# A hybrid attention block: hand order in the Fourier-projection stage, contiguous query columns for the maxima, block ends ahead on VectorE

## The chip, the cores and the metric

The kernel runs on one core of one Trainium2 chip. The metric is the device time of one execution in microseconds (us): the median of three runs before the change is 3602.55 us (3600.46 to 3602.69). The engines are called PE (TensorE; PEld is its weight loading), DVE (VectorE), ACT (ScalarE), POOL (GpSimd) and SP (SyncE, which issues nearly all DMAs).

## The reference

Two layers act on 2048 latent tokens and 256 context tokens of width 1024, in float32. Cut to what matters here:

```python
def layer(x, ctx, c, c_ctx, p, row, col, update_ctx):
    hx = rmsnorm(x, p["norm_g"]) * (1.0 + sc[:, None, :]) + sh[:, None, :]
    px = jnp.split(hx @ p["w_in"], SPLIT_IDX, axis=-1)      # ctx likewise: pc
    qa_x, ka_x, va_x, qb_x, kb_x, vb_x = attn_features(px, p, row, col)
    att_a = attend(qa_x, concat([ka_x, ka_c]), concat([va_x, va_c]))   # MLA, 4 heads
    att_b = attend(qb_x, concat([kb_x, kb_c]), concat([vb_x, vb_c]))   # GQA, 4 heads
    x_new = x + gt[:, None, :] * merge(px, att_a, att_b, p)

def attend(q, k, v):
    s = einsum("bqkgd,blkd->bkgql", q, k) * dk ** -0.5
    return einsum("bkgql,blkd->bqkgd", softmax(s), v)

def merge(parts, att_a, att_b, p):
    ya = att_a * silu(ga); yb = att_b * silu(gb)
    yc = chunk_mlp(u, vc, p) * silu(gc)
    yd = fourier(f, p["fnet_w"]) * silu(gd)          # 2-D FFT, then a matrix
    return concat([ya, yb, yc, yd]) @ p["w_out"]
```

The context tokens are updated in the first layer only, and read only context.

## The kernel before

**Projections.** A layer first runs the normed input through its projections, in two halves of the tokens (`HALVES`; the last one has token blocks 2 and 3, of 512 tokens). Matmuls are split in a high and a low part, three for each product (lines 364 to 366 and 714 to 716). The last stage of a half is `stage_f`: for each token block it multiplies two weight tiles (`load_coltile`, line 343: DMA of two pieces each on SP, cast on DVE, low part on POOL) with the input, 24 matmuls a tile, and then four times 6 matmuls by the Fourier matrix of the columns, whose results go to DRAM (`Z`).

**Attention** has 16 blocks a layer: four pairs of heads (0, 1 MLA; 2, 3 GQA) by four blocks of 512 queries. A block takes 18 steps over 128 keys. A step is 10 score matmuls (GQA 8; line 1140), exponentials on ACT (line 1148) and sums of `p` on POOL (line 1159, with the steps of the set `dve` on DVE); every third step 12 matmuls of `p` with the values (line 1126). The scores' last pair of matmuls has 33 rows: the 33rd carries the query's maximum, so that the exponential needs none. These maxima are found ahead: during block n the 18 *max units* of block n+1 run (`max_units`, line 963; `fill`). Sixteen are chunks, with 4 matmuls (GQA 2) of 128 queries by 512 keys into two PSUM banks "m" (line 976), which DVE reduces (line 988); two are tails over the 256 context keys, after which `mt` is complete for half the queries (lines 995, 1000). `row()` (line 1016) then writes `mt` as a row into the query tile `qt` by DMAs on SP.

**Order.** In attention the order on PE, DVE, POOL and ACT is that in which the code is written (`tc.manual_schedule`); elsewhere a scheduler sets it, and it sets SP's everywhere. PE, DVE, POOL, ACT and SP each run their instructions in order. The max units of a layer's first block are given to the second `stage_f` (`fill`), under the scheduler's order. Block 0's units end with the stage; block 3's units (for block 4) need the keys of pair 1, loaded by SP at that time (lines 953 to 957).

**The end of a block.** `join` adds DVE's sum to POOL's (line 1179), `fin` makes the denominators (line 1196) and sends them through DRAM, `recip` (line 1209) and `fin2` (line 1216) run on DVE steps later. In blocks 0 to 2 DVE also does the Fourier branch (`fu`, with 32 matmuls at line 854 each time). After the last block the output projection begins, whose weights and inputs share stage buffers with POOL's and DVE's work (lines 1321, 1322, 1338 to 1340).

Of the kernel before, what the change touches and what calls it, by code (L numbers as in the profile page):

```python
# [15 lines left out]
P = 128  # L16
# [20 lines left out]
def kernel(  # L37
# [49 lines left out]
    def f32(ap):  # L87
        return ap.bitcast(F32)
# [270 lines left out]
            nc.tensor.matmul(pt[:, :n], hx(0, k)[:, js], lo(k), start=False, stop=False)  # L359
            nc.tensor.matmul(pt[:, :n], hx(1, k)[:, js], hi(k), start=False, stop=(k == KD - 1))  # L360

    def feat_major(pt, hx, wt, n):
        for k in range(KD):
            nc.tensor.matmul(pt[:, :n], wt[:, 0, k, :], hx(0, k), start=(k == 0), stop=False)  # L364
            nc.tensor.matmul(pt[:, :n], wt[:, 0, k, :], hx(1, k), start=False, stop=False)  # L365
            nc.tensor.matmul(pt[:, :n], wt[:, 1, k, :], hx(0, k), start=False, stop=(k == KD - 1))  # L366
# [17 lines left out]
    def layer(l, xin, shs, hxs, xss, c):  # L384
# [300 lines left out]
                sg = silu2(pg, n, hx_p.tile([P, 512], F32, tag="t", name="sg"))  # L685
                load(G[gi][:, t0:t0 + n], sg[:, :n])

        def stage_f(hxs, blks, fill):
            left = [4 * len(blks)]

            def drain():
                k = -(-len(fill) // left[0])
                left[0] -= 1
                for u in fill[:k]:
                    u()
                del fill[:k]
            wts = [load_coltile(l, 2144 + P * i) for i in range(2)]
            for b in blks:
                t0, n = blk_tokens(b)
                fT = []  # L700
                for i in range(2):
                    pf = bank("s", [P, 512])
                    feat_major(pf, hxs[b], wts[i], n)
                    f = wk("f", [P, 2, 512], F32R, bufs=3)
                    nc.scalar.copy(f[:, 0, :n], pf[:, :n])
                    nc.vector.tensor_tensor(f[:, 1, :n], pf[:, :n], f32(f[:, 0, :n]), op=ALU.subtract)
                    fT.append(f)
                    drain()
                for j in range(n // P):
                    pz = bank("o", [P, 512])  # L710
                    js = slice(j * P, (j + 1) * P)
                    for i in range(2):
                        f, w = fT[i], c.aw
                        nc.tensor.matmul(pz, f[:, 0, js], w[:, 0, i, :], start=(i == 0), stop=False)
                        nc.tensor.matmul(pz, f[:, 0, js], w[:, 1, i, :], start=False, stop=False)
                        nc.tensor.matmul(pz, f[:, 1, js], w[:, 0, i, :], start=False, stop=(i == 1))
                    zt = wk("zt", [P, 512], bufs=3)
                    nc.scalar.copy(zt, pz)
                    load(Z[:, t0 // P + j, :], zt)
                    if j % 2 == 1 and b < 4:  # L720
                        drain()

        def fnet_load():
            zt = []
# [240 lines left out]
        def max_units(blk, qt):  # L965
# [6 lines left out]
            def mm(pm, c0, qi, s0, n):  # L972
                seq = (0, 2) if pair < 2 else (0,)
                for sel in seq:
                    for e in range(2):
                        nc.tensor.matmul(  # L976
                            pm[e][:, c0:c0 + n], qt[64 * e:64 * e + 64, sel, qi:nq:nqt],
                            kp.kk(e, sel, 64, s0, n), start=(sel == 0), stop=(sel == seq[-1]),
                        )

# [32 lines left out]
            def row():  # L1013
                for e in range(2):
                    r = 64 * e + 32
                    load(
                        f32(qt)[r:r + 1, 3 if pair < 2 else 2, :nq].rearrange("r (p x) -> r p x", x=nqt),
                        f32(mt)[:, 4 * e:4 * e + nqt],
                    )
            return units, row  # L1020

        blocks = [(pair, qb) for pair in range(4) for qb in range(4)]
# [12 lines left out]
        def merge(x, y):  # L1035
# [6 lines left out]
                i = j  # L1042
            return r + x[i:]

        for hi_, half in enumerate(HALVES):
            full = [b for b in half if not (last and b == 4)]
            wc = load_c((nc.scalar.copy, nc.vector))
            if c is None:
                c = consts(l)
            for b in half:  # L1050
                if b not in hxs:
                    hxs[b] = make_hx(b, shs, xin, xss.get(b))
            with scope(f"c{l}{hi_}"):
                stage_c(hxs, full, wc)
                if hi_ == 0:
                    make_up(l, c)
                wm = load_group(l, (0, 352), 2)
            with scope(f"m{l}{hi_}"):
                wg, pre = group_units(l, (608, 1120), 2)
                stage_mla(hxs, half, wm, pre)  # L1060
            with scope(f"g{l}{hi_}"):
                wg0 = load_coltile(l, GC[0])
                stage_gqa(hxs, half, wg)
            with scope(f"t{l}{hi_}"):
                mods, shs_next = [], None
                if hi_ == 1:
                    gt, mods = mods_b(l, 1 if last else 2)
                    if not last:
                        shs_next, more = mods_a(l + 1)
                        mods += more  # L1070
                for gi in range(6):
                    ws = mods[gi][0]() if gi < len(mods) else None
                    stage_gate(hxs, full, gi, wg0 if gi == 0 else None)
                    if ws:
                        mods[gi][1](ws)
                    if gi == 0 and hi_ == 0:
                        make_aw(l, c)
                if hi_ == 1:
                    load_kc()
                    first_max = prep_block(0)  # L1080
                    fill = first_max[2][0] + [first_max[2][1]]
                else:
                    hxs[2] = make_hx(2, shs, xin)
                    fill = []
                stage_f(hxs, full, fill)
        c.pool.__exit__(None, None, None)

        def attention():
# [148 lines left out]
            for n, (pair, qb) in enumerate(blocks):  # L1237
# [9 lines left out]
                if n >= 3:  # L1247
                    dve = {(i, 1) for i in range(0, 15, 3)}
                    if pair >= 2:
                        dve |= {(i, 1) for i in range(1, 16, 3)}  # L1250
                if n == 5:
                    load_v2()
                own, zc = [], None
                if not last and qb == 3:
                    own, zc = ctx_units(pair)
                z = main_units(blk, qt, dve)
                done = 0
                for i in range(18):
                    z.scores(i)
                    want = min(len(fill), -(-len(fill) * (i + 1) // 16))  # L1260
                    while done < want:
                        fill[done]()
                        done += 1
# [4 lines left out]
                        own.pop(0)()  # L1268
                    if i % BATCH == BATCH - 1:
                        z.sums(i)  # L1270
                        j = n * 6 + i // 3
                        mults = [m() for m in fmm]
                        fmm = []
# [6 lines left out]
                        if mults and not fu and not fmm:  # L1280
                            ffin()
                        z.sums2()
                        if i == 2 and prev:
                            prev.join()
                        if tail:
                            tail.pop(0)()
                        if i == 5 and prev:
                            prev.fin()
                            tail += prev.tail
# [9 lines left out]
            for f in prev.tail:  # L1299
                f()  # L1300

        ordered = {
            mybir.EngineType.PE, mybir.EngineType.DVE, mybir.EngineType.Pool, mybir.EngineType.Activation
        }
        banks_close()
        banks_open(f"pa{l}", s=4, m=3, o=1)
        with scope(f"a{l}"), tc.manual_schedule(engines=ordered):
# [209 lines left out]
```

## Time and profile before

| | |
|---|---|
| median of 3 runs | 3602.55 us |
| the profiled execution | 3604.51 us, its span 3602.7 us |
| PE busy | 3344.2 us (93%), PEld 2415.1 us (67%) |
| DVE, POOL, ACT busy | 1981.9 us (55%), 1862.5 us (52%), 1246.8 us (35%) |
| the chain that ended last, by engine | PE 29%, DVE 6%, DMA 2%, issue 2%, POOL 1%, ACT 1% |
| mean granted clock of PE | 0.963 |

The span is what the hardware profiler saw of one execution. Busy shares are averages over stages: PE is near full in the steady part of attention and in the projections, and leaves gaps at the seams between stages and blocks. The granted clock is 1.0 at 2.4 GHz and 0.5 at 1.2 GHz.

### The profile page before, as it was taken

What the parts mean: (1) busy time and instruction counts of PE and PEld (TensorE: products, weight loads), DVE (VectorE), ACT (ScalarE), POOL (GpSimd) and SP (SyncE); (2) the same over time, 40 slices, a digit from 0 to 9 for tenths busy, and PEclk for the clock granted to TensorE, in tenths of its full rate; (3) what the DMA queues carried; (4) which work ended last, traced back from release to release, by engine and by line L of the source; (5) the groups of instructions that cost most, each with busy time, mean ns of one, the idle gap of its engine ahead of it and who ended that gap; (6) DMA issues with size and microseconds to landing.
All of it is one profiled execution on the core that took longest, in us unless ns stands there. A gap on an engine that the chain in (4) does not pass through costs nothing. (4 is left out here: it accounts for less than half of the span.)

```text
span 3602.7 us, 50865 instructions
## 1 busy us (share of the span) xinstructions
PE 3344.2 (93%) x18572; PEld 2415.1 (67%) x18572; DVE 1981.9 (55%) x3245; ACT 1246.8 (35%) x2652; POOL 1862.5 (52%) x1680
## 2 busy tenths in 40 slices
PE   6999999898989999998998998998988999999799
PEld 4888788665656655554787876876655666555387
DVE  4374337327865678772334644372488666877421
ACT  4253325102324444443123534241133344444500
POOL 2433233205757787776335242342177778777822
PEclk9999999988999999998999999999999999999999
DMA  6154314752143120003452453156413412000332
GB/s 214 37 139 126 111 45 129 226 152 84 49 129 82 36 73 18 25 23 116 150 171 82 109 143 112 36 140 171 145 53 85 123 35 60 19 19 19 129 127 92
DMA packets 283498, 345.52 MB, mean 96 GB/s; under 512 B 46616, under 2 KB 194600, under 8 KB 278120
## 3 DMA queue, kind: packets, MB, share of 16 engines
q1 hardware_dynamic: 283248, 342.28, 32.1%
q8 instruction: 146, 2.39, 0.3%
q14 instruction: 104, 0.85, 0.1%
HBM read 235.59 MB, written 106.46 MB: 95 GB/s over the span
## 5 line engine op out<-in xcount | busy, mean ns | idle before, releaser
L1159 POOL TENSOR_TENSOR acc<-acc,p 128x512 f32<-128x512 f32 x814 | 1097.0, 1371 | 272.8 <-ACT p L1148 260.5
L1148 ACT ACTIVATE p<-ps_s 128x512 f32<-128x512 f32 x1168 | 628.6, 593 | 862.8 <-PE ps_s L1140 820.5
L988 DVE TENSOR_REDUCE s<-ps_m 128x1 f32<-128x512 f32 x1024 | 645.3, 682 | 375.7 <-PE ps_m L976 368.1
L1140 PE MATMUL ps_s<-A 64*128 64x512 f32 x4456 | 691.5, 410 | 24.5 <-ACT p L1148 17.0
L1140 PEld LDWEIGHTS ps_s<-A 64*128 64x128 f32 x4456 | 452.3, 191 | 247.8 <-issue 160.8
L976 PE MATMUL ps_m<-A 64*128 64x512 f32 (+1 forms) x1808 | 434.4, 438 | 78.1 <-DVE s L988 55.2
L1126 PE MATMUL ps_o<-p,A 128*64 128x512 f32 x2048 | 496.5, 611 | 6.1 <-ACT p L1148 6.1
L976 PEld LDWEIGHTS ps_m<-A 64*128 64x128 f32 x1808 | 336.3, 309 | 151.2 <-DVE s L988 90.7
L364 PE MATMUL ps_s<-A 128*128 128x512 f32 (+1 forms) x864 | 339.3, 393 | 16.8 <-DVE sg L398 6.8
L366 PE MATMUL ps_s<-A 128*128 128x512 f32 (+1 forms) x864 | 335.0, 388 | 7.0 <-POOL A L349 7.0
L365 PE MATMUL ps_s<-A 128*128 128x512 f32 (+1 forms) x864 | 334.9, 388 | 0.0
L1126 PEld LDWEIGHTS ps_o<-p,A 128*64 128x64 f32 x2048 | 139.5, 138 | 256.2 <-issue 207.2
L358 PE MATMUL ps_s<-A 128*128 128x256 f32 (+2 forms) x848 | 291.7, 345 | 4.2 <-ACT vst L635 1.7
L359 PE MATMUL ps_s<-A 128*128 128x256 f32 (+2 forms) x848 | 287.0, 339 | 2.1 <-POOL A L333 1.9
L360 PE MATMUL ps_s<-A 128*128 128x256 f32 (+2 forms) x848 | 284.1, 335 | 3.0 <-POOL A L314 3.0
L1159 DVE TENSOR_TENSOR st<-st,p 128x512 f32<-128x512 f32 x158 | 206.4, 1307 | 52.2 <-ACT p L1148 46.3
L1366 POOL TENSOR_TENSOR A<-A,d 128x512 f32<-128x512 f32 x68 | 89.9, 1323 | 277.3 <-DVE d L1365 262.8
L1358 PE MATMUL ps_s<-A 128*128 128x512 f32 x544 | 213.3, 392 | 2.2 <-ACT rd L1200 1.4
L1360 PE MATMUL ps_s<-A 128*128 128x512 f32 x544 | 212.7, 392 | 0.0
L1359 PE MATMUL ps_s<-A 128*128 128x512 f32 x544 | 212.7, 391 | 0.0
L364 PEld LDWEIGHTS ps_s<-A 128*128 128x128 f32 x864 | 168.3, 195 | 59.4 <-DVE sg L398 9.9
L1159 POOL TENSOR_TENSOR acc<-p 128x512 f32<-128x512 f32 (+1 forms) x72 | 97.0, 1354 | 202.5 <-ACT p L1148 145.2
(198 smaller groups left out, 4785.9 us busy)
## 6 DMA issues: line engine op xcount, KB each, us to landing
st<-in_w_in SPq DMA_DIRECT2D x144, 256.0 KB
QKA<-A SPq DMA_DIRECT2D x34, 768.0 KB
A<-in_w_mod SPq DMA_DIRECT2D x24, 1024.0 KB
A<-X SPq DMA_DIRECT2D x17, 1024.0 KB
A<-in_x SPq DMA_DIRECT2D x16, 1024.0 KB
st<-Y SPq DMA_DIRECT2D x64, 256.0 KB
A<-QKA SPq DMA_DIRECT2D x56, 256.0 KB
G<-sg SPq DMA_DIRECT2D x48, 256.0 KB
```

Of the source, the lines that this page charges most:

```text
L358: nc.tensor.matmul(pt[:, :n], hx(0, k)[:, js], hi(k), start=(k == 0), stop=False)
L359: nc.tensor.matmul(pt[:, :n], hx(0, k)[:, js], lo(k), start=False, stop=False)
L360: nc.tensor.matmul(pt[:, :n], hx(1, k)[:, js], hi(k), start=False, stop=(k == KD - 1))
L364: nc.tensor.matmul(pt[:, :n], wt[:, 0, k, :], hx(0, k), start=(k == 0), stop=False)
L365: nc.tensor.matmul(pt[:, :n], wt[:, 0, k, :], hx(1, k), start=False, stop=False)
L366: nc.tensor.matmul(pt[:, :n], wt[:, 1, k, :], hx(0, k), start=False, stop=(k == KD - 1))
L976: nc.tensor.matmul(pm[e][:, c0:c0 + n], qt[64 * e:64 * e + 64, sel, qi:nq:nqt], kp.kk(e, sel, 64, s0, n), start=(sel == 0), stop=(sel == s ...
L988: nc.vector.reduce_max(out=mx[:, qi % 2, e, ci:ci + 1], in_=pm[e], axis=AX.X)
L1126: nc.tensor.matmul(z.po[64 * e:64 * e + 64, :nq], vtile(pair, e, keys[i]), pts[e][:, :nq], start=(i == 0), stop=(i == nk - 1),)
L1140: nc.tensor.matmul(ss[e][:, :nq], kp.kk(e, sel, rows, k0, P), qt[64 * e:64 * e + rows, qi, :nq], start=(m == 0), stop=(m == len(seq) - 1),)
L1148: nc.scalar.activation(p[:, :nq], ss[e][:, :nq], AF.Exp, bias=0.0, scale=1.0)
L1159: eng.tensor_tensor(acc[:, :nq], old[0][:, :nq], p[:, :nq], op=ALU.add)
```

## The change

It has five parts. (1) The second `stage_f` becomes `stage_f_max` under `manual_schedule`: after every sixth matmul one max unit. (2) Max units take contiguous query columns as weights, not every fourth one; so `row()` writes four DMAs of 128 single elements for each head instead of one of 128 times four. (3) In block 3 the max units begin at step 3 (`late`). (4) `join` and the `tail` (`recip`, `fin2`) stand ahead of the Fourier work and of DVE's sums of the same step. (5) In the last block DVE takes 17 of the 18 sums of the second head.

```diff
-    def feat_major(pt, hx, wt, n):
+    def feat_major(pt, hx, wt, n, hook=None):
         for k in range(KD):
+            if hook and k % 2 == 1:
+                hook()
...
+        def stage_f_max(blks, fill):
+            wts = f_weights()
+
+            def hook():
+                if fill:
+                    fill.pop(0)()
+            b0, b1 = blks
+            f0 = [f_feat(b0, 0, wts), f_feat(b0, 1, wts, hook)]
+            f1 = [f_feat(b1, 0, wts, hook)]
+            for j in range(4):
+                f_z(b0, j, f0)
+                hook()
+            f1.append(f_feat(b1, 1, wts, hook))
+            for j in range(4):
+                if j < 2:
+                    hook()
+                    hook()
+                f_z(b1, j, f1)
+            while fill:
+                hook()
...
-                            pm[e][:, c0:c0 + n], qt[64 * e:64 * e + 64, sel, qi:nq:nqt],
+                            pm[e][:, c0:c0 + n], qt[64 * e:64 * e + 64, sel, qi * P:(qi + 1) * P],
...
-                    load(
-                        f32(qt)[r:r + 1, 3 if pair < 2 else 2, :nq].rearrange("r (p x) -> r p x", x=nqt),
-                        f32(mt)[:, 4 * e:4 * e + nqt],
-                    )
+                    dst = f32(qt)[r:r + 1, 3 if pair < 2 else 2, :nq].rearrange("r (x p) -> r p x", p=P)
+                    for x in range(nqt):
+                        load(dst[:, :, x:x + 1], f32(mt)[:, 4 * e + x:4 * e + x + 1])
...
-                stage_f(hxs, full, fill)
+                    with tc.manual_schedule(engines=ordered):
+                        stage_f_max(full, first_max[2][0] + [first_max[2][1]])
+                    stage_f(full)
...
+                    if n + 1 == len(blocks):
+                        dve = {(i, 1) for i in range(17)}
...
-                done = 0
+                done, late = 0, (0, 0, 0, 3)[n] if n < 4 else 0
-                    want = min(len(fill), -(-len(fill) * (i + 1) // 16))
+                    want = max(0, min(len(fill), -(-len(fill) * (i + 1 - late) // (16 - late))))
...
                         z.sums(i)
+                        if i == 2 and prev:
+                            prev.join()
+                        if tail:
+                            tail.pop(0)()
...
                         z.sums2()
-                        if i == 2 and prev:
-                            prev.join()
-                        if tail:
-                            tail.pop(0)()
```

`f_weights`, `f_feat` and `f_z` hold the same operations as the body of `stage_f` before; the first half's `stage_f` calls them under the scheduler. In the order of the program the following moves.

On PE, at the start of the second Fourier-projection stage of layer 1, before (L364 to L366 are its matmuls, L976 the max units):

```order
L365 MATMUL ps_s<-A 128x512
L366 MATMUL ps_s<-A 128x512
L976 MATMUL ps_m<-A 128x512 x14
L364 MATMUL ps_s<-A 128x512
L365 MATMUL ps_s<-A 128x512
```

and in the changed kernel (L366 to L368 the projections, L995 the max units):

```order
L995 MATMUL ps_m<-A 128x512 x4
L366 MATMUL ps_s<-A 128x512
L367 MATMUL ps_s<-A 128x512
L368 MATMUL ps_s<-A 128x512
L366 MATMUL ps_s<-A 128x512
L367 MATMUL ps_s<-A 128x512
L368 MATMUL ps_s<-A 128x512
L995 MATMUL ps_m<-A 128x512 x4
```

The 14 unit matmuls that stood together after the first 12 projection matmuls are spread, four after each six projection matmuls, and the first now stands behind 27 of them.

On PE, at the end of the same stage, before (L714 to L716 are the Fourier-matrix matmuls, L1140 the first scores):

```order
L716 MATMUL ps_o<-A,f 128x512
L714 MATMUL ps_o<-A,f 128x512
L715 MATMUL ps_o<-A,f 128x512
L716 MATMUL ps_o<-A,f 128x512
L976 MATMUL ps_m<-A 128x256 x8
L1140 MATMUL ps_s<-A 128x512 x10
L976 MATMUL ps_m<-A 128x512 x8
```

and in the changed kernel the last tail (L995 x8) and what follows it (L707 to L709 are the Fourier-matrix matmuls, 24 in all until the first scores):

```order
L995 MATMUL ps_m<-A 128x512 x4
L995 MATMUL ps_m<-A 128x256 x8
L707 MATMUL ps_o<-A,f 128x512
L708 MATMUL ps_o<-A,f 128x512
L709 MATMUL ps_o<-A,f 128x512
```

The last tail no longer stands directly before the first scores.

On SP, at the end of a GQA block of layer 1 and the start of the next one, before (L1016 writes the maxima, L1202 and L1205 move the denominators):

```order
L1218 DMA Y_2_3_17243<-rd 128x512
L1193 DMA gate<-G_3_17227 128x512
L1016 DMA A<-mt 1x128x4 x2
L1202 DMA den<-rd 2x512
L1205 DMA r_30584<-den 128x8
L1210 DMA den<-r_30584 128x8
```

and in the changed kernel (L1037 writes the maxima, L1223, L1226 and L1231 move the denominators):

```order
L1239 DMA Y_2_3_17349<-rd 128x512
L1214 DMA gate<-G_3_17333 128x512
L1037 DMA A<-mt 1x128x1 x4
L1223 DMA den<-rd 2x512
L1226 DMA r_30777<-den 128x8
L1037 DMA A<-mt 1x128x1 x4
L1231 DMA den<-r_30777 128x8
```

Eight transfers stand where two stood: four at the end of a block, and four (for the first 256 queries of the next one) in mid-block, behind the load of the denominators.

On POOL, in the last block of layer 1 and after it, before (L1159 are the sums of `p`, L1322 the low part of the output weights, L1217 the block's gate):

```order
L1159 TENSOR_TENSOR acc<-acc,p 128x512 x2
L1322 TENSOR_TENSOR A<-st,A 128x512 x3
L1159 TENSOR_TENSOR acc<-acc,p 128x512
L1322 TENSOR_TENSOR A<-st,A 128x512
L1159 TENSOR_TENSOR acc<-acc,p 128x512 x3
L1217 TENSOR_TENSOR rd<-rd,gate 128x512
L1159 TENSOR_TENSOR acc<-acc,p 128x512 x10
L1366 TENSOR_TENSOR A<-A,d 128x512
L1217 TENSOR_TENSOR rd<-rd,gate 128x512
```

and in the changed kernel (L1180 the sums, L1342 the low part, L1238 the gate):

```order
L1342 TENSOR_TENSOR A<-st,A 128x512 x3
L1180 TENSOR_TENSOR acc<-acc,p 128x512
L1342 TENSOR_TENSOR A<-st,A 128x512
L1180 TENSOR_TENSOR acc<-acc,p 128x512 x2
L1238 TENSOR_TENSOR rd<-rd,gate 128x512
L1180 TENSOR_TENSOR acc<-acc,p 128x512 x6
L1386 TENSOR_TENSOR A<-A,d 128x512
L1238 TENSOR_TENSOR rd<-rd,gate 128x512
```

The sums between the weight pieces become fewer, and the last run of sums has 6 instead of 10.

## Rows read from the trace of the kernel before

**Rows 1.** Page, part 5 (columns: engine, operands, count; busy, mean; idle): weight loads.

```profile
L1140 PEld LDWEIGHTS ps_s<-A 64*128 64x128 f32 x4456 | 452.3, 191 | 247.8 <-issue 160.8
...
L976 PEld LDWEIGHTS ps_m<-A 64*128 64x128 f32 x1808 | 336.3, 309 | 151.2 <-DVE s L988 90.7
```

**Rows 2.** Timeline (start us, us, engine, line) of PE, layer 1, a latent-attention block.

```profile
2923.64 0.63 PE L976 MATMUL ps_m<-A 64*128 64x512 f32 x4
2924.11 1.32 PE L1140 MATMUL ps_s<-A 64*128 64x512 f32 x10
...
2939.29 0.98 PE L976 MATMUL ps_m<-A 64*128 64x256 f32 x8
2940.11 2.48 PE L1140 MATMUL ps_s<-A 64*128 64x512 f32 x20
```

**Rows 3.** Timeline of PE, layer 0, context scores.

```profile
1084.65 0.76 PE L1140 MATMUL ps_s<-A 64*128 64x256 f32 x10
```

**Rows 4.** Timeline of PE, layer 1, Fourier projections to first scores.

```profile
2536.20 0.79 PE L364 MATMUL ps_s<-A 128*128 128x512 f32 x1
2536.79 0.63 PE L365 MATMUL ps_s<-A 128*128 128x512 f32 x1
2537.22 0.63 PE L366 MATMUL ps_s<-A 128*128 128x512 f32 x1
...
2538.59 0.39 PE L364 MATMUL ps_s<-A 128*128 128x512 f32 x1
...
2545.16 0.39 PE L366 MATMUL ps_s<-A 128*128 128x512 f32 x1
...
2549.03 0.85 PE L976 MATMUL ps_m<-A 64*128 64x512 f32 x2
2549.81 0.50 PE L715 MATMUL ps_o<-A,f 128*128 128x512 f32 x1
...
2590.88 1.49 PE L1140 MATMUL ps_s<-A 33*128 33x512 f32 x2 [0.43 <-DMA A<-mt]
```

**Rows 5.** Windows (us, engines' busy time, PEclk, DMA): start of layer 1's attention.

```profile
2588.00:2599.00 11.00, 9.33 (x39) 6.31 (x41) 4.71 (x9) 2.28 (x4) 1.64 (x2) 0.56 0.50 151
```

**Rows 6.** Timeline of SP, layer 1, weight loads of the Fourier projections.

```profile
2530.22 1.51 SPq L347 DMA_DIRECT2D st<-in_w_in  x3
```

**Rows 7.** Timeline of SP, layer 1, row transfers of the first block.

```profile
2588.91 1.18 SPq L1016 DMA_DIRECT2D A<-mt  x2
```

**Rows 8.** Timeline of SP, layer 0, weight loads of the Fourier projections.

```profile
759.56 0.95 SPq L347 DMA_DIRECT2D st<-in_w_in  x2
```

**Rows 9.** Timeline of PE, layer 0, first block's first step.

```profile
827.54 0.49 PE L1140 MATMUL ps_s<-A 33*128 33x512 f32 x1 [0.89 <-DMA A<-mt]
```

**Rows 10.** Timeline of PE, layer 0, start of the fourth block.

```profile
1025.51 1.42 PE L1140 MATMUL ps_s<-A 64*128 64x512 f32 x10
...
1040.41 2.76 PE L1140 MATMUL ps_s<-A 64*128 64x512 f32 x10
```

**Rows 11.** Timeline of PE, layer 1, start of the fourth block.

```profile
2778.70 1.43 PE L1140 MATMUL ps_s<-A 64*128 64x512 f32 x10
...
2788.50 2.75 PE L1140 MATMUL ps_s<-A 64*128 64x512 f32 x10
```

**Rows 12.** Timeline of all engines, layer 1, end of a grouped-query block.

```profile
3083.18 0.18 DVE L1000 TENSOR_REDUCE mt<-s 128x4 fp32r<-128x20 f32 x1
...
3083.38 1.16 SPq L1016 DMA_DIRECT2D A<-mt  x2
...
3087.32 0.40 PE L1140 MATMUL ps_s<-A,kz 33*128 33x512 f32 x2
```

**Rows 13.** Timeline of SP, layer 1, end of the fourth block.

```profile
2839.14 1.16 SPq L1016 DMA_DIRECT2D A<-mt  x2
```

**Rows 14.** Timeline of PE, layer 1, same place as [rows 13].

```profile
2844.25 0.75 PE L1140 MATMUL ps_s<-A 33*128 33x512 f32 x2 [0.52 <-DMA A<-mt]
```

**Rows 15.** Groups by line of POOL, layer 1, last block (columns as in [rows 1]).

```profile
L1159 POOL TENSOR_TENSOR acc<-acc,p 128x512 f32<-128x512 f32 x25 | 36.0, 1456 | 5.8 <-ACT p L1148 5.5
```

More of the change, by code (lines that the diff above doesn't have):

```diff
@@ L686, in stage_gate @@
                 load(G[gi][:, t0:t0 + n], sg[:, :n])
[L688 to L697, printed above, removed]
-            for b in blks:
[L699 to L721, printed above, removed]
@@ new lines, in f_weights, with f_feat, f_z @@
+        def f_weights():
+            return [load_coltile(l, 2144 + P * i) for i in range(2)]
+        def f_feat(b, i, wts, hook=None):
+            n = blk_tokens(b)[1]
+            pf = bank("s", [P, 512])
+            feat_major(pf, hxs[b], wts[i], n, hook)
+            f = wk("f", [P, 2, 512], F32R, bufs=3)
+            nc.scalar.copy(f[:, 0, :n], pf[:, :n])
+            nc.vector.tensor_tensor(f[:, 1, :n], pf[:, :n], f32(f[:, 0, :n]), op=ALU.subtract)
+            return f
+        def f_z(b, j, fT):
+            pz = bank("o", [P, 512])
+            js = slice(j * P, (j + 1) * P)
+            for i in range(2):
+                f, w = fT[i], c.aw
+                nc.tensor.matmul(pz, f[:, 0, js], w[:, 0, i, :], start=(i == 0), stop=False)
+                nc.tensor.matmul(pz, f[:, 0, js], w[:, 1, i, :], start=False, stop=False)
+                nc.tensor.matmul(pz, f[:, 1, js], w[:, 0, i, :], start=False, stop=(i == 1))
+            zt = wk("zt", [P, 512], bufs=3)
+            nc.scalar.copy(zt, pz)
+            load(Z[:, blk_tokens(b)[0] // P + j, :], zt)
@@ new lines, in stage_f @@
+        def stage_f(blks):
+            wts = f_weights()
+            for b in blks:
+                fT = [f_feat(b, i, wts) for i in range(2)]
+                for j in range(blk_tokens(b)[1] // P):
+                    f_z(b, j, fT)
+        def stage_f_max(blks, fill):
+            wts = f_weights()
+            def hook():
[15 more added lines that the diff above has]
+                hook()
@@ L1043, in merge @@
             return r + x[i:]
+        ordered = {
+            mybir.EngineType.PE, mybir.EngineType.DVE, mybir.EngineType.Pool, mybir.EngineType.Activation
+        }
         for hi_, half in enumerate(HALVES):
@@ L1080, in layer @@
                     first_max = prep_block(0)
-                    fill = first_max[2][0] + [first_max[2][1]]
+                    with tc.manual_schedule(engines=ordered):
+                        stage_f_max(full, first_max[2][0] + [first_max[2][1]])
                 else:
                     hxs[2] = make_hx(2, shs, xin)
-                    fill = []
-                stage_f(hxs, full, fill)
+                    stage_f(full)
         c.pool.__exit__(None, None, None)
@@ L1300, in attention @@
                 f()
-        ordered = {
-            mybir.EngineType.PE, mybir.EngineType.DVE, mybir.EngineType.Pool, mybir.EngineType.Activation
-        }
         banks_close()
```

## The prediction

> **What bounds the kernel now.** I read the page first: PE is busy for 93% of the span, the other engines for 55% or less, so the time is PE's, and what can be won is its gaps, its exposed weight loads and its half-clock stretches. Then I read PE's timeline where the change acts. Inside a latent-attention block there are no gaps to win: four unit matmuls take 0.47 us from their start to the next scores, 0.235 a pair [rows 2]. The seams are another thing. In the Fourier-projection stage PE runs projection matmuls at 0.43 us each (1.2 GHz) where the full clock gives 6.57 us for 29, or 0.227 [rows 4]. At the fourth block's start two score steps, with two units between them, lie 14.90 us apart in layer 0 and 9.80 in layer 1 [rows 10, 11]. SP's timeline shows two row transfers at a block's end [rows 12], POOL's groups 25 sums of `p` in the last block [rows 15].
>
> The profiled execution took 3604.5 us, 2 us more than the median. The sum is made against 3604.5 and 2 us are taken off at the end.
>
> **Part 1, the Fourier-projection stage.** Its end is the 33-row pair of scores that needs the maxima: 2590.88 in layer 1, 827.54 in layer 0, both ended by the row's transfer [rows 4, 9]. In the changed order PE must wait for weights early on, since the units that filled that wait stand later. In layer 1 SP issues three pieces at 2530.22, and the projections went on at 2536.20, with reductions between the casts [rows 4, 6]; I take 5.5 us from the first issue to the first usable piece, so 2535.7. From there:
> - 132 of the stage's 144 projection and Fourier-matrix matmuls (12 need only the first piece): 132 x 0.227 = 30.0 us.
> - 16 chunk units. The cheapest a unit can be is 2 x 0.235 = 0.47. At the dearest, one strided pair between Fourier-matrix matmuls takes 0.78 from start to start, and about 0.09 ahead of its start, so a unit of two pairs takes 0.87 + 0.235 = 1.1 [rows 4]. With contiguous weights, whose mean load is 0.19 us and not 0.31 [rows 1], I take 0.9: 14.4 us. Two tails at 1.1: 2.2 us.
> - Clock: the wait ahead will lower it as before; 12 matmuls at 0.43 instead of 0.227 give 2.4, I take 2.7.
> - Four pairs of scores: 0.93.
>
> That is 2585.9, 5 us earlier than 2590.88 (3 if a unit costs 1.1; 8 with 0.65 and a full clock). In layer 0 the two pieces are issued at 759.56 [rows 8], so usable at 765.1; 120 matmuls are left (27.2), and with the same other terms the 33-row pair comes at 812.5, 15 us earlier (10 to 18). The row's transfer is not late: in layer 1 two issues and their landing took the 2.0 us from 2588.91 to 2590.88 [rows 4, 7], so four take some 3.1; now 24 matmuls (5.4 us) and 0.9 of scores lie between the last tail and the pair, which leaves 3.2 for the last reductions. It just fits. Term: -20, bounds -13 and -26.
>
> **The clock after it.** The first 11 us of layer 1's attention have a granted clock of 0.56, hence mostly 1.2 GHz, after PE had stood idle between the last tail and the first scores [rows 5]. That pause goes. At full clock 9.3 us of busy PE would shrink by up to 4, but in that block DVE's Fourier work ends many waits, so -2 a layer: -4, bounds 0 and -8.
>
> **Part 2, contiguous columns.** All 1944 unit loads get cheaper by about 0.12 us, together 0.23 ms of PEld [rows 1]. Nearly all of it lies beside matmuls: a strided pair of 512 columns takes 0.235, no more than the contiguous score pairs, of which 20 matmuls and their end take 2.48 [rows 2]. What counts are pairs too short to hide a load. The tail's four pairs of 256 columns take 0.82 [rows 2]; ten contiguous matmuls of that width take at most 0.76 with their end, some 0.12 a pair [rows 3], so a tail of four falls to 0.47: 0.35 saved. A layer has 14 MLA tails in attention, and 16 GQA tails of two pairs, of which I take 0.12 each. PE sets the pace in blocks 4 to 15, less so in 0 to 3, so 8 x 0.35 + 16 x 0.12 = 4.7 a layer; with small gains elsewhere -10, bounds -4 and -15.
>
> **The row's transfers** are the price. Before, two issue over 1.16 us from 0.02 after `mt` is ready (3083.36), and the 33-row pair runs at 3087.32 without waiting, 3.96 after `mt` [rows 12]. Four issues take twice as long: the last one starts some 1.8 us after `mt` rather than 0.6. By layer 1's first row, a transfer lands about 1.4 us after its issue starts [rows 4, 7], which would be at 3.2; from the slow case, where the second was issued at about 2839.7 and PE waited until 2844.25 [rows 13, 14], it takes 4.5, which would be at 6.3 and so 2.3 late. Of the 32 rows most stand in quiet stretches, a few behind key loads as in the slow case. I take +1.2 us for six of them: +7, bounds 0 and +20. The other four transfers are issued in mid-block; on SP they stand behind the denominators' load and ahead of their store back, and have half a block of slack.
>
> The Trainium skill speaks against this edit: its page "DMA: Bandwidth & Descriptors", section "Rules for kernel authors", says to join many small transfers into one large one, as small ones are mostly overhead. No run here has 4-byte rows, so the trace neither bears it out nor refutes it; by it the transfers would tend to the slow end, which is the rival "rows late" below.
>
> **Part 3, late units in block 3.** From one score step to the next, the trace has 14.90 and 9.80 us [rows 10, 11]. A step with two units needs 5 x 0.23 + 4 x 0.235 = 2.1, so 12.8 and 7.7 are waits for keys and half clock. The first unit now comes after three steps, a drain of 12 matmuls (2.7) and Fourier matmuls, near 12 us after the block's start, when the keys are there in layer 1 and short by 1 to 2 us in layer 0. Eighteen units over 13 steps make five steps double, about 1 us a layer on DVE. Term: -(20.5 - 1.5 - 2) = -17; bounds -8 (if DVE, not PE, holds that block) and -21.
>
> **Part 4** takes nothing off PE: `recip` and `fin2` release SP's transfers and POOL's gate earlier, `join` releases `fin` some steps later anyway. What is queued behind them on DVE are its sums, by which no bank waits. 0, bounds -2 and +2.
>
> **Part 5, the last block.** POOL gives up eight of 25 sums of 1.456 us [rows 15], 11.7 us; between them stand the weight pieces that free the stage buffers for the next output weights. DVE takes them on, which is busy for 55% of the span. If POOL alone held the block, a layer would gain 11.7, plus the final run's four sums in part; if the transfers' landing holds it, 0. I take -6 in layer 1 and -5 in layer 0, where the end hangs on the context block's denominators, which don't change: -11, bounds -2 and -18.
>
> **Sum.** -20 - 4 - 10 + 7 - 17 + 0 - 11 = -55: 3549.5 against 3604.5, hence 3548 against the median.
>
> **Rivals.**
> *Gains given back.* Blocks 0 to 3 are paced by DVE's Fourier work, so that an earlier start of block 0 is spent waiting there; the late units make block 3 DVE-bound; the last block stays bound by transfers. For it: DVE fills those blocks more than PE's gaps show. Against it: the Fourier work is counted in steps, and so starts earlier as well. Stage -12, clock 0, columns -5, row +7, block 3 -9, last block -4: -23, so 3580.
> *Rows late.* One mechanism, at every one of 32 boundaries: 4-byte transfers that land as slowly as in rows 13 and 14, or all eight placed at the end because SP's mid-block place is blocked. The first gives 1.8 + 4.5 - 4.0 = 2.3 late, 74 us, and instead of -62 in the other terms the time would be some 3614. With both, the last one starts at 3.9 and lands at 8.4: 4.4 late, 141 us, 3681. It decides from 2 us a boundary on, above which the kernel is slower. For it: twice eight issues on SP at a seam where 1.4 us were spare. Against it: the usual landing is short [rows 4, 7]. Price taken: 3620.
> *The clock stays up.* If the early wait in the stage doesn't lower the clock and the last block loses its half-clock stretches as well, stage -26, clock -8, columns -13, row 0, block 3 -20, last block -16: -83, so 3520.
> *It doesn't do what it says.* If units stay as dear in the hand order as the strided ones and wait for DVE at each place, part 1 gives nothing: 3568, inside the main range.
>
> **How the numbers follow.** Chances: the forecast 0.66, gains given back 0.21, rows late 0.06, clock up 0.07. The range, 3520 to 3585, holds the forecast's bounds but their far ends, the second case and half of the fourth; what is left out are rows late, half of the clock case and the tail of the second, below 0.2. Faster and slower are counted from 0.2% on, 7 us, about what a measurement of this kernel can tell from no change. Slower needs rows late (0.04 of its 0.06); no change comes from the rest of it and from the worst ends of the second case: 0.04. Faster: 0.92.
>
> **What would show it.** In the changed profile: PE without waits for `QKA` at the stage's start and with its first score step directly behind the Fourier-matrix matmuls, the 33-row pairs near 2586 and 812; unit loads at 0.19 us mean; tails of 0.5 us; block 3 with its first two score steps under 2 us apart; waits of the 33-row pairs for `mt` below 10 us in sum (rows late would show them at 2 us and more at each boundary); POOL's last run of sums six long, and PE's half clock in the last block less. Wrong would make me: idle PE at block starts ended by `mt`, or waits of the same length moved behind DVE in blocks 0 to 3.

## The result and the profile after

The changed kernel takes 3550.33 us (median of 4 runs, 3549.66 to 3551.26) against 3602.62 in the same session: a ratio of 0.9856, interval [0.9839, 0.9873], 52 us faster. The forecast was 3548. Its profiled execution took 3549.66 us with a span of 3547.9, 54.8 us shorter than before.

The same matmuls of PE and the same writes of `mt` can be looked up in both traces, since their counts are equal. Their times give where the 54.8 us went (us, both layers together):

| stretch | forecast | measured |
|---|---|---|
| start of the kernel to the Fourier-projection stage of layer 0 | 0 | -5.0 |
| Fourier-projection stages, to the first 33-row pair | -20 | -19.9 |
| rest of block 0 | -4 | -6.6 |
| blocks 1 and 2 | 0 | -3.6 |
| block 3 | -17 | -17.2 |
| blocks 4 to 7 (MLA) | -5.6 of columns, some of the rows | -5.1 |
| blocks 8 to 14 (GQA) | -3.8 of columns, some of the rows | +15.0 |
| block 15 to the output projection | -11 | -9.9 |
| layer 0's output projection to layer 1's stage | 0 | -2.5 |

The last row and the first are scatter: in the runs below, whose instructions there are the same, the first stretch lies between 6.8 us shorter and 2.7 longer than before.

**The unit loads** fell as forecast, from a mean of 309 ns to 190 [rows 1], by the page's groups:

```profile
L1161 PEld LDWEIGHTS ps_s<-A 64*128 64x128 f32 x4456 | 435.4, 188 | 255.6 <-issue 159.5
...
L995 PEld LDWEIGHTS ps_m<-A 64*128 64x128 f32 x1808 | 214.9, 190 | 183.0 <-DVE s L1007 142.7
```

**The stage in layer 1**, PE's timeline:

```profile
2493.78 0.79 PE L366 MATMUL ps_s<-A 128*128 128x512 f32 x1 [5.25 <-DVE A L348]
2494.37 0.63 PE L367 MATMUL ps_s<-A 128*128 128x512 f32 x1
...
2499.57 0.74 PE L995 MATMUL ps_m<-A 64*128 64x512 f32 x4
...
2501.84 0.73 PE L995 MATMUL ps_m<-A 64*128 64x512 f32 x4
...
2534.94 0.94 PE L995 MATMUL ps_m<-A 64*128 64x512 f32 x5
2537.01 0.74 PE L995 MATMUL ps_m<-A 64*128 64x256 f32 x7 [1.13 <-DVE s L1007]
...
2544.26 1.42 PE L1161 MATMUL ps_s<-A 64*128 64x512 f32 x10 [0.72 <-ACT zt L711]
```

PE waits 5.25 us for a cast, as the units that stood there are gone; then eight matmuls run at the lower clock, most of them at 0.43 us from start to start as in [rows 4], and from 2499.57 on there is one unit every 2.25 us. A unit takes 0.66 us from its start to the next projection matmul, but the matmuls around it are spaced wider too: 2.25 less six matmuls of 0.227 leaves 0.89 for a unit, as the 0.9 assumed. There is one wait for the reductions, 1.13 us at the last tail, and one of 0.72 us for a copy on ACT (L711) ahead of the first scores. These come at 2544.26 without waiting for the maxima, and the 33-row pair 1.03 us later without waiting for the row. The clock, by windows (span, then busy time of PE, PEld, DVE, ACT, POOL, then the clock):

```profile
2544.00:2555.00 11.00, 10.11 (x70) 6.28 (x72) 8.08 (x10) 3.47 (x7) 5.62 (x4) 1.00 0.65 216
```

Where it had been 0.56 [rows 5] it is 1.00.

**The fourth block** of layer 0, PE's timeline: three score steps without units, the Fourier matmuls and the drain, where PE had waited for keys [rows 10]. Of that wait 1.02 us is left behind them, as the keys are still short there (the forecast had 1 to 2 us).

```profile
999.37 4.09 PE L1161 MATMUL ps_s<-A 64*128 64x512 f32 x30
1003.39 3.84 PE L873 MATMUL ps_m<-A 128*128 128x128 f32 x32
1007.16 2.80 PE L1147 MATMUL ps_o<-p,A 128*64 128x512 f32 x12
...
1012.57 0.96 PE L995 MATMUL ps_m<-A 64*128 64x512 f32 x4 [1.02 <-DMA A<-QKA]
```

**The row's transfers** at a GQA block's end, on all engines:

```profile
3116.46 0.18 DVE L1019 TENSOR_REDUCE mt<-s 128x4 fp32r<-128x20 f32 x1
...
3116.66 3.07 SPq L1037 DMA_DIRECT2D A<-mt  x4
...
3121.27 0.47 PE L1161 MATMUL ps_s<-A,kz 33*128 33x512 f32 x1 [0.18 <-DMA A<-mt]
```

Four issues take 3.07 us where two took 1.16 [rows 12]. The second 33-row matmul starts 4.63 us after `mt` is ready instead of 3.96 for the pair, with a wait of 0.18 put down to `mt`. In sum PE's matmuls wait for `mt` about as long as before (waits: us in total, times, longest; before, then after):

```profile
PE ps_s L1140 <- DMA A<-mt: 4.5, 8, 1.0
```

```profile
PE ps_s L1161 <- DMA A<-mt: 4.7, 8, 1.6
```

Those of the layers' first blocks [rows 4, 9] are gone, and others have come.

**What the forecast did not have** is the 15 us in the GQA blocks. Before, in mid-block (DVE's timeline, then POOL's):

```profile
3159.34 3.19 DVE L1159 TENSOR_TENSOR st<-st,p 128x512 f32<-128x512 f32 x2
3162.46 0.68 DVE L1216 TENSOR_TENSOR rd<-rd,po 128x512 f32<-128x512 f32 x1
3163.06 3.07 DVE L988 TENSOR_REDUCE s<-ps_m 128x1 f32<-128x512 f32 x5
```

```profile
3156.30 5.68 POOL L1159 TENSOR_TENSOR acc<-acc,p 128x512 f32<-128x512 f32 x4 [3.03 <-ACT p L1148]
3163.22 1.28 POOL L1217 TENSOR_TENSOR rd<-rd,gate 128x512 f32<-128x512 f32 x1 [1.23 <-DVE rd L1216]
```

DVE adds its two sums (L1159) while POOL adds its own; POOL then stops for `fin2` (L1216), since its next instruction is the product of `fin2`'s result and the gate. So `fin2` runs beside an idle POOL and takes 0.68 us. After the change:

```profile
3148.80 1.51 DVE L1237 TENSOR_TENSOR rd<-rd,po 128x512 f32<-128x512 f32 x1
3150.24 3.47 DVE L1180 TENSOR_TENSOR st<-st,p 128x512 f32<-128x512 f32 x2
3153.62 2.47 DVE L1007 TENSOR_REDUCE s<-ps_m 128x1 f32<-128x512 f32 x4
```

```profile
3145.77 5.69 POOL L1180 TENSOR_TENSOR acc<-acc,p 128x512 f32<-128x512 f32 x4 [2.81 <-ACT p L1169]
3151.42 1.73 POOL L1238 TENSOR_TENSOR rd<-rd,gate 128x512 f32<-128x512 f32 x1
3153.12 3.08 POOL L1180 TENSOR_TENSOR acc<-acc,p 128x512 f32<-128x512 f32 x2
```

`fin2` (L1237), moved ahead of the sums, runs beside POOL's adds and takes 1.51 us. POOL does not have to stop any more, and the sums behind `fin2` run beside it to their end (3.47 us for two instead of 3.19). The reductions start 4.82 us after `fin2`'s start, where sums and `fin2` together took 3.72 before. PE waits for them:

```profile
3154.36 0.49 PE L995 MATMUL ps_m<-A 64*128 64x512 f32 x1 [1.46 <-DVE s L1007]
...
3199.50 0.49 PE L995 MATMUL ps_m<-A 64*128 64x512 f32 x1 [1.48 <-DVE s L1007]
...
3201.19 4.36 PE L1147 MATMUL ps_o<-p,A 128*64 128x512 f32 x12
```

In this block it waits 1.46 us. In the next one the wait is followed by 12 value matmuls that take 4.36 us instead of 2.79, at a granted clock of 0.66 (columns as in [rows 5]):

```profile
3201.00:3206.00 5.00, 5.00 (x17) 1.62 (x18) 3.91 (x5) 0.88 (x2) 3.28 (x3) 0.66 0.00 0
```

Of the fourteen blocks 8 to 14 of both layers, twelve have such a wait of 1.45 to 1.50 us, and behind three of them the 12 value matmuls take 4.4 to 4.5 us, each time at a granted clock of 0.66. Of the other two, one (wait 0.64 us) shows the same contest with the other outcome, on DVE and on POOL:

```profile
3104.60 0.68 DVE L1237 TENSOR_TENSOR rd<-rd,po 128x512 f32<-128x512 f32 x1
```

```profile
3101.87 6.23 POOL L1180 TENSOR_TENSOR acc<-acc,p 128x512 f32<-128x512 f32 x4 [3.10 <-ACT p L1169]
```

There `fin2` takes 0.68 us although POOL adds beside it, and POOL's four adds take 6.23 us instead of 5.69.

### The profile page after: what moved, and what is told of

The parts are those of the page before. It is cut to its first block, busy times and chain, and to the rows that moved or that the text cites. A ratio compares the mean times of both kernels' runs of the same rounds, so it can differ in the third digit from the quotient of the medians.

```text
span 3547.9 us, 51161 instructions
## 1 busy us (share of the span) xinstructions
PE 3274.5 (92%) x18572; PEld 2297.1 (65%) x18572; DVE 2010.1 (57%) x3259; ACT 1247.8 (35%) x2652; POOL 1865.4 (53%) x1666
## 5 line engine op out<-in xcount | busy, mean ns | idle before, releaser
L1180 POOL TENSOR_TENSOR acc<-acc,p 128x512 f32<-128x512 f32 x802 | 1087.7, 1379 | 306.0 <-ACT p L1169 294.8
L1161 PE MATMUL ps_s<-A 64*128 64x512 f32 x4456 | 674.5, 407 | 21.0 <-ACT p L1169 15.8
L1161 PEld LDWEIGHTS ps_s<-A 64*128 64x128 f32 x4456 | 435.4, 188 | 255.6 <-issue 159.5
L995 PE MATMUL ps_m<-A 64*128 64x512 f32 (+1 forms) x1808 | 369.9, 399 | 87.5 <-DVE s L1007 85.0
L366 PE MATMUL ps_s<-A 128*128 128x512 f32 (+1 forms) x864 | 340.2, 394 | 29.1 <-DVE A L348 19.6
L368 PE MATMUL ps_s<-A 128*128 128x512 f32 (+1 forms) x864 | 333.6, 386 | 7.1 <-POOL A L349 7.0
L995 PEld LDWEIGHTS ps_m<-A 64*128 64x128 f32 x1808 | 214.9, 190 | 183.0 <-DVE s L1007 142.7
L1180 DVE TENSOR_TENSOR st<-st,p 128x512 f32<-128x512 f32 x172 | 232.0, 1349 | 20.1 <-ACT p L1169 13.1
L366 PEld LDWEIGHTS ps_s<-A 128*128 128x128 f32 x864 | 167.2, 194 | 78.5 <-DVE A L348 22.5
L349 POOL TENSOR_TENSOR A<-st,A 128x512 fp32r<-128x512 f32 x64 | 84.8, 1336 | 213.6 <-DVE A L348 175.8
```

Of the source, the lines that this page charges most:

```text
L995: nc.tensor.matmul(pm[e][:, c0:c0 + n], qt[64 * e:64 * e + 64, sel, qi * P:(qi + 1) * P], kp.kk(e, sel, 64, s0, n), start=(sel == 0), stop ...
L1161: nc.tensor.matmul(ss[e][:, :nq], kp.kk(e, sel, rows, k0, P), qt[64 * e:64 * e + rows, qi, :nq], start=(m == 0), stop=(m == len(seq) - 1),)
L1180: eng.tensor_tensor(acc[:, :nq], old[0][:, :nq], p[:, :nq], op=ALU.add)
```

## The experiments

Ratios are to the kernel before, run in the same session; the median before lay between 3604 and 3607 us there.

**Part 4 undone.** `join` and the `tail` go back behind `sums2`:

```diff
                         z.sums(i)
-                        if i == 2 and prev:
-                            prev.join()
-                        if tail:
-                            tail.pop(0)()
...
                         z.sums2()
+                        if i == 2 and prev:
+                            prev.join()
+                        if tail:
+                            tail.pop(0)()
```

> The changed kernel with its part 4 undone: join, recip and fin2 stand behind the Fourier work and the sums of their step on DVE, as before. Theory A (the order on DVE): in the changed kernel fin2, ahead of the sums, runs beside POOL's adds, takes 1.35 us instead of 0.68, and delays the reductions, so that PE waits 1.2 us more in each of some 16 GQA blocks and now and then falls to half clock; undone, about 18 us come back there, and perhaps 6 us that the early order won in blocks 0 to 2 are lost: 3538 us (3533 to 3543), GQA blocks 43.9 to 44.0 us long instead of 44.56. Rival B (the rows): the GQA blocks are longer because eight row transfers end later than two; the order on DVE does nothing: 3550 us (3547 to 3553).

Measured: 3540.56 us against 3607.28, ratio 0.9816 [0.9802, 0.9829]; the changed kernel's is 0.9856 to 0.9860, so about 15 us came back. Blocks 8 to 14 are 20.9 us shorter than in the changed kernel, blocks 1 and 2 some 4.8 longer. Theory A holds, B falls. PE's wait of 1.45 to 1.50 us in these blocks is 0.36 to 0.40 us in the repeat of this kernel, and no value matmuls there run at the lower clock: about 13 and 5 of the 20.9 us. The blocks' `fin2`, by groups of lines over five GQA blocks (a repeat of this kernel):

```profile
L1237 DVE TENSOR_TENSOR rd<-rd,po 128x512 f32<-128x512 f32 x6 | 4.1, 680 | 0.0
```

and in the changed kernel, with the reductions:

```profile
L1007 DVE TENSOR_REDUCE s<-ps_m 128x1 f32<-128x512 f32 x154 | 94.6, 680 | 39.7 <-PE ps_m L995 39.7
...
L1237 DVE TENSOR_TENSOR rd<-rd,po 128x512 f32<-128x512 f32 x5 | 6.7, 1348 | 0.0
```

`fin2` takes 680 ns against a mean of 1348, in which four take 1.51 to 1.53 us and the one shown above 0.68; the reductions take 680 in both.

**Only `join` ahead**: as above, but with the two lines of `join` left in their new place.

> The changed kernel with join left ahead of the sums, but recip and fin2 back behind them. Theory A: all of the loss is fin2's; join ahead costs 0.4 us more and the first sum behind it 0.55 less, so the time is that of the kernel with part 4 undone, near 3538 us, within 3 us of it. If join's place matters, it lies 3 us or more from it. Rival B: 3550 us (3547 to 3553).

Measured: 3540.68 us, 0.12 us from the kernel with all of part 4 undone, and blocks 8 to 14 are shorter than in the changed kernel by the same 20.9 us. The loss is that of the `tail`; for `join`'s place no effect is seen, with four runs that lie between 3534 and 3548.

**Part 2 undone**, and **strided columns with eight transfers**:

```diff
-                            pm[e][:, c0:c0 + n], qt[64 * e:64 * e + 64, sel, qi * P:(qi + 1) * P],
+                            pm[e][:, c0:c0 + n], qt[64 * e:64 * e + 64, sel, qi:nq:nqt],
...
-                    dst = f32(qt)[r:r + 1, 3 if pair < 2 else 2, :nq].rearrange("r (x p) -> r p x", p=P)
+                    dst = f32(qt)[r:r + 1, 3 if pair < 2 else 2, :nq].rearrange("r (p x) -> r p x", x=nqt)
```

That is the edit for eight transfers; with part 2 undone `row()` is the old one, with two.

> The changed kernel with part 2 undone: max units read every fourth query column, and two transfers of 16-byte elements write a row. Theory A: columns cost 8 to 12 us again, chiefly tails of 256 columns and the units in the Fourier-projection stage, and the rows give back 0.3 to 0.5 us at some 25 boundaries, 8 to 12 us: 3551 us (3545 to 3557). Rival B: the rows give back 15 us and more: 3543 us or less.

> The changed kernel with strided query columns, but the row still written by eight transfers of 4-byte elements (each element now goes to every fourth place). Against the kernel with strided columns and two transfers it shows the price of the eight transfers alone, against the changed kernel that of the columns alone. Theory A: 3560 us (3555 to 3566), rows 8 to 12 us, columns 8 to 12 us. Rival B: rows 15 us or more, so 15 us above the kernel with two transfers.

Measured: 3579.07 us and 3584.39 us against 3607.28, ratios 0.9923 [0.9910, 0.9935] and 0.9939 [0.9926, 0.9953]. The eight transfers cost 5.3 us (forecast 7; every run with eight lies above every run with two, by 1 to 13 us), and they are not what lengthens the GQA blocks: with two transfers (and strided columns) blocks 8 to 14 are 19.7 us longer than before the change, with eight 21.8. The columns are worth 0.9939 - 0.9860 = 0.0079, 28 us, where every theory had 8 to 12. About 9 of them lie in the two Fourier-projection stages, the others in attention. A reason shows in the unit matmuls of five GQA blocks, before the change, after it, and in the changed kernel with strided columns and eight transfers (groups by line):

```profile
L976 PE MATMUL ps_m<-A 64*128 64x512 f32 x160 | 53.2, 442 | 4.9 <-DVE s L988 4.9
...
L976 PE MATMUL ps_m<-kb,A 64*128 64x256 f32 x40 | 6.3, 364 | 0.0
```

```profile
L995 PE MATMUL ps_m<-A 64*128 64x512 f32 x154 | 45.0, 420 | 11.4 <-DVE s L1007 10.9
...
L995 PE MATMUL ps_m<-kb,A 64*128 64x256 f32 x40 | 4.6, 293 | 0.0
```

```profile
L995 PE MATMUL ps_m<-A 64*128 64x512 f32 x154 | 52.1, 446 | 9.6 <-DVE s L1007 9.6
...
L995 PE MATMUL ps_m<-kb,A 64*128 64x256 f32 x40 | 6.3, 364 | 0.0
```

Not only the tails' matmuls (364 to 293 ns) but also the 512-column ones get shorter, 442 to 420, and with the columns alone put back both are as long as before. The difference is largest where a 512-column matmul has waited for a bank: there the mean is 0.62 us with strided columns and 0.50 with contiguous ones, while the first matmul of a unit that has not waited takes 0.41 and 0.40.

**Part 1 undone**: the old `stage_f` under the scheduler, all else as changed.

```diff
-                    with tc.manual_schedule(engines=ordered):
-                        stage_f_max(full, first_max[2][0] + [first_max[2][1]])
+                    fill = first_max[2][0] + [first_max[2][1]]
...
+                stage_f(hxs, full, fill)
```

> The changed kernel with part 1 undone: the Fourier-projection stage is the old one, ordered by the scheduler, all else as changed. Theory A (the stage's gain is its hand order, less what contiguous columns alone give it): 10 to 14 us slower than the changed kernel, 7 to 10 of it in layer 0, and the half clock at the start of attention is back (about 3 us more). Rival B: the contiguous columns alone would have given most of it: under 6 us slower.

Measured: 3576.66 us against 3556.68 for the changed kernel in the same session (its repeat is below): 20.0 us slower, more than either theory had. Between the two profiles, which differ by 14.0 us in all, 9.3 are lost before the first scores and 9.6 from there to the end of block 0, 3.4 of these up to the 33-row pair; later stretches give some back. PE's timeline at the first scores of layer 0, and the windows at those of both layers:

```profile
816.50 1.18 PE L1144 MATMUL ps_s<-A 64*128 64x512 f32 x8 [1.47 <-DVE s L997]
819.21 0.76 PE L1144 MATMUL ps_s<-A 33*128 33x512 f32 x1 [1.53 <-DMA A<-mt]
```

```profile
816.00:827.00 11.00, 8.00 (x35) 5.38 (x37) 3.70 (x7) 2.28 (x4) 0.77 (x1) 0.61 0.42 117
2561.00:2572.00 11.00, 7.58 (x46) 5.43 (x46) 4.55 (x8) 2.62 (x5) 1.29 (x2) 0.84 0.52 157
```

The scores again wait for the last reductions and then for the row, 1.5 us each. The clock is not at 1.00 but at 0.61 and 0.84. So what comes behind the last tail is worth about as much as the close packing ahead of it. That the tail's place, 24 matmuls ahead of the scores, is the reason is read from these waits; no run moves the tail alone.

**Part 3 undone**:

```diff
-                done, late = 0, (0, 0, 0, 3)[n] if n < 4 else 0
+                done, late = 0, 0
```

> The changed kernel with part 3 undone: the max units of block 3 begin at step 0 again. Theory A: PE waits for the keys of pair 1 as before, 17 us slower than the changed kernel (13 to 20). Rival B: the wait only moves, since blocks 0 to 3 now come earlier against the key loads, or it is DVE that holds block 3: under 8 us slower.

Measured: 3575.56 us, 18.9 us slower than the changed kernel. In its profile, which is the fastest of six runs between 3562 and 3581, block 3 is 14.7 us longer. PE's timeline in layer 1 has the wait back, and longer than before the change (there 3.84 and 1.33 us), presumably as the block now comes earlier against its keys:

```profile
2738.99 1.44 PE L1161 MATMUL ps_s<-A 64*128 64x512 f32 x10
2745.63 0.76 PE L995 MATMUL ps_m<-A 64*128 64x512 f32 x1 [5.20 <-DMA A<-QKA]
2747.71 1.33 PE L995 MATMUL ps_m<-A 64*128 64x512 f32 x4 [1.32 <-DMA A<-QKA]
```

**Part 5 undone**:

```diff
-                    if n + 1 == len(blocks):
-                        dve = {(i, 1) for i in range(17)}
```

> The changed kernel with part 5 undone: in the last block POOL adds again what DVE had taken. Theory A: 8 to 11 us slower than the changed kernel, all of it in the last block of each layer. Rival B: the last blocks gain by part 4 (join ahead) and not by part 5: under 4 us slower.

Measured: 3569.99 us, 13.3 us slower, more than theory A had. In its profile the last blocks account for only 4.9 us (1.6 and 3.3); that profile is the fastest of its four runs, which lie between 3564 and 3574. So part 5 is worth 5 to 13 us, and more is not settled. POOL's adds in layer 1's last block, with part 5 undone and in the changed kernel (groups by line; a few records are missing from each):

```profile
L1180 POOL TENSOR_TENSOR acc<-acc,p 128x512 f32<-128x512 f32 x28 | 40.0, 1447 | 7.6 <-ACT p L1169 7.5
```

```profile
L1180 POOL TENSOR_TENSOR acc<-acc,p 128x512 f32<-128x512 f32 x22 | 31.1, 1427 | 9.9 <-ACT p L1169 9.6
```

**The changed kernel again:**

> The changed kernel once more, on the chip of the three kernels that each undo one part, so that differences are taken on one chip. All theories: 0.9855 of the kernel before, within 0.002.

Measured: 3556.68 us against 3607.03, ratio 0.9860 [0.9847, 0.9872].

**POOL idle at `fin2`**: does `fin2` slow down because POOL adds beside it? This kernel leaves out POOL's sums of steps 9 to 11 in the GQA blocks, so it does not compute the reference; it serves for the times alone.

```diff
                         for e, p in enumerate(pts):
+                            if pair >= 2 and i in (9, 10, 11) and (i, e) not in dve:
+                                continue
...
-                    nc.scalar.copy(z.rd[:, :nq], pd[:, :nq])
+                    nc.scalar.activation(z.rd[:, :nq], pd[:, :nq], AF.Identity, bias=ones[:, 0:1], scale=1.0)
```

> The changed kernel, but in GQA blocks POOL leaves out its sums of p of steps 9 to 11 (one is added to the denominators so that they stay finite). So POOL is idle or nearly so when fin2 and the sums behind it run on DVE, in the changed order. Theory A1 (an add on DVE is slow only while POOL adds): fin2 falls from 1.35 to about 0.7 us in these blocks, the sums next to it too, and PE's wait of 1.2 to 1.5 us for the reductions behind it goes: 12 to 22 us under the changed kernel. Rival A2 (fin2 is long for its own place, by what it waits for or by its operands): it stays at 1.3 us or more and the wait stays: under 5 us.

Measured: 3535.12 us against 3604.39, ratio 0.9810 [0.9791, 0.9829], 18 us under the changed kernel. DVE's timeline and POOL's, same place:

```profile
3097.95 0.68 DVE L1239 TENSOR_TENSOR rd<-rd,po 128x512 f32<-128x512 f32 x1
3098.55 2.38 DVE L1180 TENSOR_TENSOR st<-st,p 128x512 f32<-128x512 f32 x2
3100.91 3.68 DVE L1007 TENSOR_REDUCE s<-ps_m 128x1 f32<-128x512 f32 x6
```

```profile
3098.71 1.66 POOL L1240 TENSOR_TENSOR rd<-rd,gate 128x512 f32<-128x512 f32 x1 [6.60 <-DVE rd L1239]
3101.41 5.69 POOL L1180 TENSOR_TENSOR acc<-acc,p 128x512 f32<-128x512 f32 x4 [1.05 <-ACT p L1169]
```

With the order of the changed kernel `fin2` (L1239) takes 0.68 us, as POOL has nothing to add. The two sums take 2.38 us instead of 3.47, and the reductions start 2.96 us after `fin2`, not 4.82. A1 holds by these durations. The time says less: blocks 8 to 14 are 29.9 us shorter than in the changed kernel, 9 more than with part 4 undone, so something else in this kernel saves time too, probably the sums that are left out. The Trainium skill has this rule: "SBUF — State Buffer", section "Who interferes with whom", says that a VectorE instruction with two SBUF inputs contends with a GpSimd instruction that reads SBUF, and a reduction does not. The traces agree, with 0.68 against 1.51 us for `fin2` at the places shown and 0.68 for the reductions in every kernel. The prediction did not weigh that rule.

**Part 4 in blocks 0 to 3 alone**, as the experiments point to, beside the kernel with part 4 undone:

```diff
+                def block_end(i):
+                    if i == 2 and prev:
+                        prev.join()
+                    if tail:
+                        tail.pop(0)()
...
                         z.sums(i)
-                        if i == 2 and prev:
-                            prev.join()
-                        if tail:
-                            tail.pop(0)()
+                        if n < 4:
+                            block_end(i)
...
                         z.sums2()
+                        if n >= 4:
+                            block_end(i)
```

> The changed kernel with part 4 kept in blocks 0 to 3 of a layer alone; from block 4 on join, recip and fin2 stand behind the sums again. Theory A: 14 us of the GQA blocks come back as with part 4 undone, and the 4 to 5 us that the early order won in blocks 1 to 3 stay: 17 to 20 us under the changed kernel, 3 to 5 us under the kernel with part 4 undone. Rival: what differs in blocks 1 to 3 between those profiles is scatter, and the time is that of the kernel with part 4 undone within 2 us.

> The kernel with part 4 undone once more, for the comparison with the one that keeps part 4 in blocks 0 to 3, on one chip. All theories: 0.9816 of the kernel before, within 0.002.

Measured: 3536.62 us (0.9812 [0.9794, 0.9831]) and 3539.22 us (0.9819 [0.9804, 0.9835]). Both beat the changed kernel by 13 to 17 us (by its ratio of 0.9856 to 0.9860) and the kernel before by 65 to 68. Between them 2.6 us is within their scatter, so the times do not settle it. The profiles do show blocks 1 and 2 shorter by 6.2 us in the first.

## Why the prediction was right, and where it was not

- **The stages** (-20): right in size, 19.9 (14.5 in layer 0, 5.4 in layer 1), and a unit cost the 0.9 assumed. Two errors offset each other. In layer 1 the weights came in 9.1 us after the stage's start (2493.78 against 2484.64), about 1.7 earlier than assumed; against that stood two waits that the sum did not have, 1.13 us at the last tail and 0.72 for ACT ahead of the first scores.
- **The clock after it** (-4): the clock went from 0.56 to 1.00 as said. Block 0 gained 6.6 beyond the 33-row pair, and the hand order accounts for it: with the old stage 6.2 us of that are lost again. The step "DVE's Fourier work ends many waits, so -2 a layer" was too cautious.
- **Contiguous columns** (-10 beside the stage): mechanism right, size wrong. Undone they cost 28 us, about 19 of them outside the stage. The failed step is "What counts are pairs too short to hide a load"; 512-column matmuls gained as well, most of all those behind a wait for a bank. The tails themselves did as forecast: four pairs that took 0.82 us [rows 2] take 0.47 (990.08 to 990.55 in the changed trace).
- **The row's transfers** (+7): 5.3. The usual landing was short, as the first row of layer 1 had said, and "rows late" did not come. The advice of the Trainium skill ("DMA: Bandwidth & Descriptors", section "Rules for kernel authors") to join small transfers points the right way, at a price of 5.3 us here.
- **Late units** (-17): 17.2 in block 3, and 18.9 by the run (14.7 in block 3 of its profile).
- **Part 4** ("takes nothing off PE", 0, -2 to +2): wrong. It costs 15 us. The step "What is queued behind them on DVE are its sums, by which no bank waits" stopped one short: behind the sums stand the reductions, for which PE waits, and the move made `fin2` twice as long because POOL works beside it.
- **Part 5** (-11): 9.9 in the profile, 5 to 13 by the runs.

That the sum came within 2 us is in part luck: the columns' surplus of some 18 us and the 15 us of part 4 cancelled, and 7.5 of the profile's 54.8 us lie in stretches that the change does not touch. "Gains given back" was wrong in its places: blocks 0 to 3 kept what the stage had won.

## What to carry to other kernels

Before an instruction is moved ahead on one engine, look at what the other engine does at the new moment: an add may have been cheap where it stood only because the neighbour was waiting for it. When a stage ends in a dependence (last maxima, row, scores), put independent work behind its last producer instead of packing all of it ahead. Judge a change with several parts by undoing each one: here four parts gained and one lost 15 us, which the total did not show.

## What was not expected of the hardware

An addition of two 128x512 tiles on DVE takes 0.68 us alone and up to 1.8 us beside POOL's additions; in one block it took 0.68 there too, and four of POOL's additions took 0.54 us longer. A delay of POOL by one dependence can hide this or show it. A weight load of 64x128 elements takes 0.19 us from contiguous columns and 0.31 from every fourth, and although PE loads beside its matmuls the difference was worth 28 us in 1944 loads. Three times in the changed kernel a wait of PE of 1.5 us in a full GQA block was followed by 12 matmuls that took 1.6 us more than usual; the granted clock in 5 us around them was 0.66 each time.
